# A decoder trunk on one core: the expert stage's candidate sums, selection steps, last U tiles, Gelu product and norm affine are issued in another way

## The chip, the cores and the metric

The kernel runs on one core of one Trainium2 chip. The metric is the device time of one execution in microseconds (us). A core has TensorE (matrix products, PE), VectorE (DVE), ScalarE (ACT), GpSimd (POOL) and the queues of SyncE (SP), which here issue the loads; each takes its own instructions in order.

## The reference

Two layers; x is 256 tokens by 1024 channels. In each layer two token mixers come first, then a feed-forward stage of 16,384 experts of one neuron each (PEER). The change touches the latter and the layer norm behind it:

```python
q = (h @ w_pq).reshape(B, S, PEER_HEADS, 2, half)             # 8 heads, two halves
s1, s2 = (einsum('bshd,hnd->bshn', q[..., i, :], sub_keys[i]) for i in (0, 1))   # 128 keys each
v1, i1 = lax.top_k(s1, 16);  v2, i2 = lax.top_k(s2, 16)
cand = v1[..., :, None] + v2[..., None, :]                    # 16 x 16 sums
top, pos = lax.top_k(cand, 16);  gates = softmax(top)
act = gelu(einsum('btd,bthkd->bthk', h, peer_u[idx]))         # idx: the 16 pairs' experts
y = einsum('bthk,bthkd->btd', gates * act, peer_v[idx])
x = layer_norm(ALPHA * x + y * gt2, ln_g, ln_b)
```

(The first lines are drawn together from several of the reference.)

## The kernel before

The kernel gathers nothing: it multiplies h by all of peer_u and takes gates that are zero but for the chosen experts. It holds fp32 accuracy by splitting every operand in two (h and lo, `wh` and `wl`) and adding three products. `peer` does this in four stages a layer.

- **U.** `u_tile(j)` for the 128 tiles of 128 experts: 24 products of 128x256 into a bank `A`, two tiles to a bank, two banks. `take` fetches, turns and splits tiles ahead. A tile is turned in one of two ways: a `u` tile by a stream transpose on VectorE (L220), an `x` tile by eight transposes on TensorE into bank `T` (L251), which ScalarE then copies twice over. In `uv_seq` every fourth tile is an `x`. Then ScalarE writes `wh` (L58) and GpSimd the rest, `wl` (L271).
- **Top-k, beside U.** `topk` is a generator: `pull`, behind each tile, lets it issue work of a given cost (1.55 a tile, 2.75 behind an x tile). For each of 16 units (a head, a block of 128 tokens) `key_ops` finds the 16 largest of two rows of 128 scores, and `cand_ops` of the unit before, interleaved with it, adds the two lists (L1400, 64 and 48 sums that can matter) and finds the 16 largest sums. The scores come through bank `K`, copied by ScalarE one unit ahead. Then the selection (L1444 to L1488) turns positions into expert numbers and gates, for each block of tokens, with operations on 128x2048 elements (L1465, L1468, L1470) twice.
- **Placement, beside U.** `place_gates`, in 64 blocks of four tokens: `build` compares (L1499) and multiplies (L1504) on VectorE, `prod` makes eight products into a bank `G`, `put` lays them into the expert-by-token buffer: a copy by ScalarE where the Gelu values are not there yet, a product by VectorE where they are (L1531). `fin_u` does the rest: it writes Gelu values of a finished pair of tiles, and where gates already stand multiplies by them (L1618).
- **V.** For the 128 tiles of peer_v VectorE and ScalarE split the gated values (`o`) and the weights, TensorE adds into four `Y` banks. In this stage GpSimd loads the norm's gain and bias (L434) and applies them to x, as two operations of 128x1024 for each half of the tokens (L1727, L1728).

The schedule is the order in which the Python issues instructions; no planner reorders it.

## Time and profile before

| | us |
|---|---|
| median of 3 runs (2248.74 to 2251.46) | 2249.8 |
| profiled execution | 2254.38 |
| its span | 2252.6 |
| TensorE busy | 2135.2 (95%) |
| VectorE busy | 1817.2 (81%) |
| ScalarE busy | 1172.5 (52%) |
| GpSimd busy | 1041.5 (46%) |

Busy shares are means over stages with different limits, so the stages are read one by one. In layer 0 U starts at about 303 us and V at 777; in layer 1 at about 1407 and 1883. A matmul's record overlaps the next one, so the pace of the products is read from their starts.

### The profile page before, as it was taken

Reading aid. Unit: us, or ns where it says so; the run is one execution under the profiler, and the core shown is the slowest. Engines: PE = TensorE matmul, PEld = TensorE weight load, DVE = VectorE, ACT = ScalarE, POOL = GpSimd, SP = SyncE. Lnnn points to the kernel's source line nnn. Section 1 sums busy time; section 2 is a strip of 40 time slices with the busy share of each in tenths; the row PEclk is TensorE's granted clock in tenths of the full one; section 3 lists DMA queues with packets and bytes.
Section 4 is the critical chain, followed back from the end, with each engine's and each line's share of the span. In section 5 each row is a group of like instructions: output and inputs, shape, how many; then the busy total and the mean of one; then the engine's idle time right before and its main releaser. Section 6 shows DMA issues by size and latency. Waiting matters only on the chain.

```text
span 2252.6 us, 42211 instructions
## 1 busy us (share of the span) xinstructions
PE 2135.2 (95%) x14596; PEld 1945.4 (86%) x14596; DVE 1817.2 (81%) x3278; ACT 1172.5 (52%) x2445; POOL 1041.5 (46%) x760
## 2 busy tenths in 40 slices
PE   5789899899999999999989998998999999999998
PEld 5789799899999978888779897997999999788886
DVE  7887989999997488888887558999999955666675
ACT  3446555455555545555545564554555555455562
POOL 4656637787778510000045534577777783200001
PEclk8999999999999999999999999999999999999999
DMA  8646567666667678888844335675766676666662
GB/s 273 196 137 221 159 140 159 129 148 148 142 147 156 176 236 275 281 286 283 298 134 150 113 121 142 147 153 118 154 142 148 146 164 187 202 196 192 193 227 90
DMA packets 498895, 400.32 MB, mean 178 GB/s; under 512 B 291920, under 2 KB 446072, under 8 KB 498680
## 3 DMA queue, kind: packets, MB, share of 16 engines
q1 hardware_dynamic: 496936, 392.33, 62.8%
q0 software_dynamic: 1408, 4.23, 0.6%
q8 instruction: 115, 1.88, 0.3%
q10 hardware_dynamic: 336, 1.06, 0.1%
q14 instruction: 100, 0.82, 0.1%
HBM read 396.46 MB, written 1.05 MB: 176 GB/s over the span
## 4 chain that ended last, share of the span: by engine, by line
PE 73%; DVE 16%; DMA 4%; issue 3%; ACT 3%; POOL 1%; SPq 1%; POOLq 0%; ACTq 0%; DVEq 0%
PE A L61 28%; PE Y L61 27%; PE T L61 7%; PE G L61 4%; PE T L251 2%; DVE wl L271 2%; PE ss L61 2%; PE hs L61 2%; DMA raw<-in_peer_u_dram 2%; POOL wl L271 1%; DVE qk L857 1%; DMA raw<-in_peer_v_dram 1%; DVE raw L220 1%; DVE e L843 1%; DVE o L1504 1%
## 5 line engine op out<-in xcount | busy, mean ns | idle before, releaser
L271 POOL TENSOR_TENSOR wl<-raw,wh 128x512 fp32r<-128x512 f32 x663 | 914.3, 1406 | 700.9 <-ACT wh L58 582.4
L58 ACT ACTIVATE wh<-raw 128x512 fp32r<-128x512 f32 x1060 | 610.8, 623 | 182.0 <-PE A L61 47.6
L61 PE MATMUL A<-hTh,wh 128*128 128x256 f32 x2080 | 543.3, 293 | 11.9 <-ACT wh L58 11.8
L61 PE MATMUL A<-hTl,wh 128*128 128x256 f32 x2080 | 524.2, 284 | 0.0
L61 PE MATMUL Y<-wh,o 128*128 128x512 f32 x1776 | 480.5, 392 | 0.8 <-DVE o L521 0.8
L271 DVE TENSOR_TENSOR wl<-raw,wh 128x512 fp32r<-128x512 f32 x525 | 380.2, 765 | 63.5 <-ACT wh L58 44.9
L61 PEld LDWEIGHTS A<-hTh,wh 128*128 128x128 f32 x2080 | 400.6, 193 | 14.4 <-ACT wh L58 13.7
L61 PEld LDWEIGHTS A<-hTl,wh 128*128 128x128 f32 x2080 | 401.7, 193 | 0.8 <-DVE hTl L521 0.2
L61 PEld LDWEIGHTS Y<-wh,o 128*128 128x128 f32 x1776 | 334.9, 189 | 70.8 <-DVE o L521 1.2
L61 PE MATMUL A<-hTh,wl 128*128 128x256 f32 x2080 | 337.9, 285 | 11.0 <-POOL wl L271 10.9
L61 PEld LDWEIGHTS A<-hTh,wl 128*128 128x128 f32 x2080 | 288.9, 193 | 14.2 <-POOL wl L271 14.2
L61 PE MATMUL Y<-wl,o 128*128 128x512 f32 x888 | 277.9, 393 | 10.4 <-DVE wl L271 10.4
L220 DVE STREAM_TRANSPOSE raw<-raw 128x1024 f32<-128x1024 f32 x192 | 235.1, 1230 | 11.7 <-DMA raw<-in_peer_u_dram 10.1
L58 ACT ACTIVATE o<-buf 128x256 fp32r<-128x256 f32 x228 | 95.1, 417 | 282.7 <-PE Y L61 282.7
L521 DVE TENSOR_TENSOR o<-buf,o 128x256 fp32r<-128x256 f32 x228 | 100.1, 439 | 150.4 <-ACT o L58 150.4
L61 PEld LDWEIGHTS Y<-wl,o 128*128 128x128 f32 x888 | 168.1, 189 | 48.9 <-DVE wl L271 13.8
L1499 DVE TENSOR_TENSOR o<-iT,iota_t 128x1024 f16<-128x1024 f16 x128 | 163.9, 1280 | 0.0
L58 ACT ACTIVATE buf<-G 128x128 f32<-128x128 f32 (+4 forms) x244 | 56.0, 276 | 203.6 <-PE G L61 203.6
L570 POOL TENSOR_TENSOR x<-x,buf 128x1024 f32<-128x1024 f32 x1 | 2.4, 2392 | 291.0 <-DVE x L567 291.0
L61 PE MATMUL T<-hTh,wh 128*128 128x256 f32 x512 | 133.6, 293 | 0.0
L61 PE MATMUL T<-hTl,wh 128*128 128x256 f32 x512 | 130.1, 286 | 0.0
L1504 DVE TENSOR_TENSOR o<-gT,o 128x1024 f16<-128x1024 f16 x128 | 124.6, 973 | 4.4
(496 smaller groups left out, 3254.9 us busy)
## 6 DMA issues: line engine op xcount, KB each, us to landing
raw<-in_peer_u_dram SPq DMA_DIRECT2D x1024, 128.0 KB, 3.5
raw<-in_peer_v_dram SPq DMA_DIRECT2D x256, 512.0 KB, 4.4
raw<-in_w_in_dram SPq DMA_DIRECT2D x88, 512.0 KB, 4.9
raw<-in_w_ada_dram SPq DMA_DIRECT2D x78, 512.0 KB, 4.9
raw<-in_w_o_dram SPq DMA_DIRECT2D x16, 512.0 KB, 3.5
raw<-in_w_pq_dram SPq DMA_DIRECT2D x64, 128.0 KB, 3.4
qk<-in_w_ada_dram SPq DMA_DIRECT2D x10, 512.0 KB, 3.9
e<-in_w_ada_dram SPq DMA_DIRECT2D x8, 512.0 KB, 6.0
```

Of the source, the lines that this page charges most:

```text
L58: nc.scalar.activation(o, i, f, **kw)
L61: nc.tensor.matmul(o, a, b, start=start, stop=stop, **kw)
L220: nc.vector.transpose(t, t)
L251: nc.tensor.transpose(banks[s][:, q], t[:, (4 * s + q) * P:(4 * s + q + 1) * P], ident)
L271: eng.tensor_sub(lo, src, h.bitcast(F32))
L521: nc.vector.tensor_sub(lo, src, h.bitcast(F32))
L570: nc.gpsimd.tensor_mul(xt[tt], xt[tt], last[0])
L843: eng.tensor_sub(ev[:, :, :hn], mid, bv[:, :, :hn])
L857: nc.vector.tensor_mul(tv[:, :, hn:], nodes(qT, n)[:, :, hn:], ev[:, :, hn:])
L1499: nc.vector.tensor_tensor(o.rearrange("p a u n v -> p (a u) n v"), iT[:, b].rearrange("p a (u v) -> p (a u) v", v=2)[:, :, None] .to_broad ...
L1504: nc.vector.tensor_mul(og.rearrange("p u a n v -> p (u a) n v"), gT[:, b * nu:(b + 1) * nu].rearrange("p u a v -> p (u a) v")[:, :, None] ...
```

## The change

Five edits, all in or beside `peer`:

1. `cand_ops` has ScalarE copy the first list of 16 values into a PSUM tile `vp` (a bank of `G`, taken when the search begins), and the additions read it there instead of in SBUF.
2. The selection yields after single operations, with higher costs, so that fewer of them are issued behind one tile.
3. `x` tiles end at tile 100: tiles 103, 107, ... 127 become `u` tiles, seven a layer.
4. `fin_u` of a finished pair is issued behind the `pull` of the even tile instead of ahead of it.
5. GpSimd's two times two operations on x become sixteen of 128x256, written behind V tiles 38 to 53.

```diff
-    uv_seq = [("x" if j % 4 == 3 else "u", j) for j in range(NK)] + [("v", j) for j in range(NK)]
+    uv_seq = [("x" if j % 4 == 3 and j < 100 else "u", j) for j in range(NK)] + [("v", j) for j in range(NK)]
...
+                    vp = psk.tile([P, 2, PH, TOPK], F32, name="G")
...
+                        act(vp[:, tt, h], v[0][tt][:, h], AF.Copy)
+                        yield 0.0
                         for a0, a1, w in segs:
...
-                                                 v[0][tt][:, h, a0:a1, None].to_broadcast(dims),
+                                                 vp[:, tt, h, a0:a1, None].to_broadcast(dims),
...
                             nc.vector.tensor_scalar(sel[a].bitcast(U32), puf, 4 - 2 * a, None,
                                                     op0=OP.logical_shift_right)
+                            yield 0.5
                             nc.vector.tensor_copy(half[2 + a], iu[a][tt].rearrange("p h k -> p (h k)").bitcast(U32))
+                            yield 0.6
...
-                        yield 0.9
+                        yield 0.5
...
-                            yield 1.4
+                            yield 1.7
                             nc.vector.tensor_mul(m, m, per_head(half[2 + a])[:, :, None].to_broadcast(k4))
                             yield 1.1
                             nc.vector.tensor_reduce(per_head(sel[a]), m, axis=mybir.AxisListType.X, op=OP.add)
-                            yield 1.4
+                            yield 1.6
...
-                    if pend:
-                        fin_u(*pend.pop())
                     if j % 2 == 1:
                         pend.append((j - 1, ps))
...
                     u_tile(j)
+                    old = [pend.pop(0)] if len(pend) > j % 2 else []
                     pull(sides, 1.55 + 1.2 * (kind == "x"))
+                    for f in old:
+                        fin_u(*f)
...
-                    if j in (NB_J + 6, NB_J + 12):
-                        xb = from_blocks(xt[j // 6 - (NB_J + 6) // 6])
-                        nc.gpsimd.tensor_mul(xb, xb, in_blocks(g_row))
-                        nc.gpsimd.tensor_add(xb, xb, in_blocks(b_row))
+                    n = j - NB_J - 6
+                    if 0 <= n < 16:
+                        xb = from_blocks(xt[n // 8])[:, n % 4]
+                        (nc.gpsimd.tensor_add if n // 4 % 2 else nc.gpsimd.tensor_mul)(
+                            xb, xb, in_blocks(b_row if n // 4 % 2 else g_row)[:, n % 4])
```

The first place is VectorE in the search of layer 0, around one unit's additions (`buf_3125` is the buffer with scores, lists and sums, `G` the bank with the copied list). Before:

```order
L1384 MAX buf_3125<-buf_3125 128x8
L1400 TENSOR_TENSOR buf_3125<-buf_3125 128x64
L1384 MAX buf_3125<-buf_3125 128x8
L1400 TENSOR_TENSOR buf_3125<-buf_3125 128x48
L1387 MAX_INDEX buf_3125<-buf_3125 128x8
```

Both additions read SBUF alone here. In the changed kernel, on the same engine at the same place:

```order
L1386 MAX buf_3125<-buf_3125 128x8 x2
L1404 TENSOR_TENSOR buf_3125<-G,buf_3125 128x64
L1389 MAX_INDEX buf_3125<-buf_3125 128x8
L1404 TENSOR_TENSOR buf_3125<-G,buf_3125 128x48
L1389 MAX_INDEX buf_3125<-buf_3125 128x8
```

The additions keep their places but for one operation, and read `G`. The copy that they wait for stands on ScalarE, in the same stretch, behind the score copy (`buf_3125<-K`) and sometimes behind the next tile's `wh`:

```order
L58 ACTIVATE buf_3125<-K 128x256
L58 ACTIVATE buf_3123<-A 128x512
L58 ACTIVATE wh<-raw 128x4x4x32 x2
L58 ACTIVATE G<-buf_3125 128x16
L58 ACTIVATE wh<-raw 128x4x4x32 x2
L58 ACTIVATE buf_3125<-K 128x256
L58 ACTIVATE G<-buf_3125 128x16
```

The row `G<-buf_3125` is new; the Gelu values (`buf_3123<-A`) now stand behind the score copy.

The second place is VectorE in the selection of layer 0, its first half, with the stream transposes of the U tiles between. Before:

```order
L1453 TENSOR_SCALAR buf_3125<-buf_3125 128x128
L1455 CAST buf_3125<-buf_3125 128x128
L1453 TENSOR_SCALAR buf_3125<-buf_3125 128x128
L1455 CAST buf_3125<-buf_3125 128x128
L1457 SCALAR_TENSOR_TENSOR buf_3125<-buf_3125 128x128
L1460 SCALAR_TENSOR_TENSOR buf_3125<-buf_3125 128x128 x2
L1461 SCALAR_TENSOR_TENSOR buf_3125<-buf_3125 128x128
L220 STREAM_TRANSPOSE raw<-raw 128x1024
L1465 TENSOR_TENSOR buf_3125<-buf_3125,iota_k 128x2048
L1468 TENSOR_TENSOR buf_3125<-buf_3125 128x2048
L1470 TENSOR_REDUCE buf_3125<-buf_3125 128x128
L220 STREAM_TRANSPOSE raw<-raw 128x1024
```

No transpose stands within the small operations, and none within the three large ones. In the changed kernel, on the same engine from the same operation on:

```order
L1457 TENSOR_SCALAR buf_3125<-buf_3125 128x128
L1460 CAST buf_3125<-buf_3125 128x128
L220 STREAM_TRANSPOSE raw<-raw 128x1024
L1457 TENSOR_SCALAR buf_3125<-buf_3125 128x128
L1460 CAST buf_3125<-buf_3125 128x128
L1463 SCALAR_TENSOR_TENSOR buf_3125<-buf_3125 128x128
L1467 SCALAR_TENSOR_TENSOR buf_3125<-buf_3125 128x128 x2
L220 STREAM_TRANSPOSE raw<-raw 128x1024
L1469 SCALAR_TENSOR_TENSOR buf_3125<-buf_3125 128x128
L1473 TENSOR_TENSOR buf_3125<-buf_3125,iota_k 128x2048
L1476 TENSOR_TENSOR buf_3125<-buf_3125 128x2048
L220 STREAM_TRANSPOSE raw<-raw 128x1024
```

One transpose now stands within the small operations, one behind them, and one within the large ones. From the end of the search to the first block's comparison there were 11 transposes and 15 tiles, now there are 14 and 19; the last block's products come behind tile 105 before, behind tile 110 now.

The third place is VectorE in the placement, from the transpose of an even tile on. Before:

```order
L220 STREAM_TRANSPOSE raw<-raw 128x1024
L1618 TENSOR_TENSOR buf_3124<-A,buf_3124 128x2x76
L1499 TENSOR_TENSOR o_6590<-iT,iota_t 128x1024
L1504 TENSOR_TENSOR o_6592<-gT,o_6590 128x1024
L1531 TENSOR_TENSOR buf_3123<-G,buf_3123 128x32x4
L1531 TENSOR_TENSOR buf_3124<-G,buf_3124 128x30x4
```

The product (L1618) stands ahead of the block's comparison (L1499). In the changed kernel, some blocks on, on the same engine:

```order
L220 STREAM_TRANSPOSE raw<-raw 128x1024
L1507 TENSOR_TENSOR o_6771<-iT,iota_t 128x1024
L1512 TENSOR_TENSOR o_6773<-gT,o_6771 128x1024
L1539 TENSOR_TENSOR buf_3123<-G,buf_3123 128x32x4
L1539 TENSOR_TENSOR buf_3124<-G,buf_3124 128x30x4
L1626 TENSOR_TENSOR buf_3124<-A,buf_3124 128x2x80
```

The product that reads the bank `A` moved from the front of the block to its end. On GpSimd the sixteen pieces follow one another with no other instruction between them, behind the two loads of gain and bias, and wait for those loads only.

## Rows read from the trace of the kernel before

**Rows 1.** Windows of 100 us: the stretch, its length, then each engine's busy time with its instructions, TensorE's granted clock as a share of full speed, the share of the DMA engines and GB/s. In order: the search's end and the selection of layer 0, its placement, the end of its U stage, and the search's end and the selection of layer 1.

```profile
400.00:500.00 100.00, 90.67 (x739) 87.86 (x739) 97.08 (x158) 48.70 (x100) 77.27 (x53) 0.97 0.65 138
...
600.00:700.00 100.00, 99.83 (x929) 97.66 (x928) 97.98 (x147) 54.95 (x146) 77.71 (x56) 1.00 0.64 144
700.00:800.00 100.00, 99.97 (x759) 95.69 (x759) 51.70 (x73) 54.19 (x105) 61.14 (x48) 1.00 0.70 175
...
1500.00:1600.00 100.00, 88.50 (x713) 85.23 (x711) 97.86 (x171) 47.76 (x96) 74.23 (x52) 0.97 0.64 132
```

**Rows 2.** Windows of 20 us in the selection, of layer 0 and of layer 1, with the same columns.

```profile
420.00:440.00 20.00, 15.55 (x98) 14.52 (x97) 19.83 (x14) 8.80 (x15) 14.64 (x9) 0.83 0.36 80
...
1520.00:1540.00 20.00, 12.51 (x80) 11.06 (x79) 19.72 (x22) 8.42 (x16) 12.18 (x7) 0.91 0.35 88
...
1560.00:1580.00 20.00, 18.55 (x141) 18.05 (x140) 19.80 (x19) 9.37 (x17) 17.18 (x12) 0.91 0.52 114
```

**Rows 3.** Windows early in the V stage, of layer 0 and of layer 1, with the same columns.

```profile
826.00:836.00 10.00, 7.91 (x29) 6.08 (x28) 9.73 (x10) 4.36 (x9) 4.08 (x3) 0.85 0.83 269
836.00:846.00 10.00, 6.46 (x21) 4.65 (x20) 9.75 (x7) 1.46 (x3) 6.39 (x3) 0.84 0.43 145
...
1935.00:1950.00 15.00, 10.26 (x37) 7.50 (x36) 12.40 (x10) 4.34 (x9) 10.01 (x6) 0.86 0.50 144
```

**Rows 4.** Timeline of ScalarE and of VectorE in layer 0 (start, duration, engine, line, operation, output and inputs, shapes, count; in brackets the idle time before it and what ended it): three score copies, then the first maximum of the search, two candidate additions, the first operation of the selection and the first comparison of the placement.

```profile
320.05 0.38 ACT L58 ACTIVATE buf<-K 128x256 f32<-128x256 f32 x1 [3.56 <-PE K L61]
...
329.97 0.38 ACT L58 ACTIVATE buf<-K 128x256 f32<-128x256 f32 x1 [3.10 <-PE K L61]
...
400.71 0.38 ACT L58 ACTIVATE buf<-K 128x256 f32<-128x256 f32 x1 [1.12 <-PE K L61]
...
321.47 0.44 DVE L1384 MAX8 buf<-buf 128x8 f32<-128x128 f32 x2
...
327.66 0.23 DVE L1400 TENSOR_TENSOR buf<-buf 128x64 f32<-128x64 f32 x1
...
398.94 0.69 DVE L1400 TENSOR_TENSOR buf<-buf 128x64 f32<-128x64 f32 x1
...
416.27 0.13 DVE L1444 COPY buf<-buf 128x8 f32<-128x8 f32 x1
...
470.62 0.64 DVE L1499 TENSOR_TENSOR o<-iT,iota_t 128x1024 f16<-128x1024 f16 x1
```

**Rows 5.** VectorE in the search of layer 0: groups by form between 320 and 420 us (busy us, mean ns), then all 32 candidate additions (minimum, median and maximum of their durations in ns), then the timeline: one addition on VectorE, the pair of subtractions on GpSimd at that time, and a product of Gelu values and gates later on.

```profile
L220 DVE STREAM_TRANSPOSE raw<-raw 128x1024 f32<-128x1024 f32 x20 | 24.5, 1225 | 0.0
...
L1400 DVE TENSOR_TENSOR buf<-buf 128x48 f32<-128x48 f32 x16 | 12.3, 768 | 0.0
...
L1400 DVE TENSOR_TENSOR buf<-buf 128x64 f32<-128x64 f32 x16 | 7.7, 481 | 0.0
...
L1400 DVE TENSOR_TENSOR buf<-buf x32: 178/380/1306, 324.0 to 412.1; 128x64 f32<-128x64 f32 x16, 128x48 f32<-128x48 f32 x16
...
339.36 1.27 DVE L1400 TENSOR_TENSOR buf<-buf 128x64 f32<-128x64 f32 x1
...
338.01 2.54 POOL L271 TENSOR_TENSOR wl<-raw,wh 128x512 fp32r<-128x512 f32 x2 [0.42 <-ACT wh L58]
...
478.16 0.17 DVE L1618 TENSOR_TENSOR buf<-A,buf 128x8 f32<-128x8 f32 x1 [0.34 <-ACT A L58]
```

**Rows 6.** The chain of work that ended last, in the last U tiles of layer 0, where no placement runs (start, duration, engine, tile and line, matmuls): 96 products are four tiles, and the x tile's transposes lie between two rows.

```profile
709.29 11.51 PE A L61 x96
721.68 11.51 PE A L61 x96
```

**Rows 7.** Timeline in the selection of layer 0: TensorE at the first tile that it waits for, two operations on 2048 elements on VectorE, and GpSimd's subtractions.

```profile
418.19 0.39 PE L61 MATMUL A<-hTh,wh 128*128 128x256 f32 x1 [2.24 <-ACT wh L58]
...
422.02 2.24 DVE L1465 TENSOR_TENSOR buf<-buf,iota_k 128x2048 f16<-128x2048 f16 x1
...
450.55 1.18 DVE L1468 TENSOR_TENSOR buf<-buf 128x2048 f16<-128x2048 f16 x1
...
430.81 14.71 POOL L271 TENSOR_TENSOR wl<-raw,wh 128x512 fp32r<-128x512 f32 x10 [3.19 <-ACT wh L58]
```

**Rows 8.** Timeline in the placement of layer 0: on TensorE the products of three blocks (four tiles lie between the first and the second), on VectorE a product of Gelu values and gates and the second half of the build behind it.

```profile
602.51 0.63 PE L61 MATMUL G<-o,o 128*128 128x128 f16 x8
...
617.13 0.63 PE L61 MATMUL G<-o,o 128*128 128x128 f16 x8
...
620.72 0.63 PE L61 MATMUL G<-o,o 128*128 128x128 f16 x8
...
617.54 0.44 DVE L1618 TENSOR_TENSOR buf<-A,buf 128x312 f32<-128x312 f32 x1
...
619.00 1.67 DVE L1504 TENSOR_TENSOR o<-gT,o 128x1024 f16<-128x1024 f16 x1
```

**Rows 9.** Timeline early in the V stage of layer 0: GpSimd's first operation on x, and three pairs of subtractions on VectorE.

```profile
828.91 2.37 POOL L1727 TENSOR_TENSOR x<-x,buf 128x1024 f32<-128x1024 f32 x1
...
827.98 3.85 DVE L271 TENSOR_TENSOR wl<-raw,wh 128x512 fp32r<-128x512 f32 x2
...
832.09 1.28 DVE L271 TENSOR_TENSOR wl<-raw,wh 128x512 fp32r<-128x512 f32 x2
...
837.40 5.62 DVE L271 TENSOR_TENSOR wl<-raw,wh 128x512 fp32r<-128x512 f32 x2
```

More of the change, by code (lines that the diff above doesn't have):

```diff
@@ L1454, in topk @@
                                                     op0=OP.logical_shift_right)
+                            yield 0.5
                             nc.vector.tensor_copy(half[2 + a], iu[a][tt].rearrange("p h k -> p (h k)").bitcast(U32))
+                            yield 0.6
                         nc.vector.scalar_tensor_tensor(half[0], sel[1].bitcast(U32), -12.0, sel[0].bitcast(U32),
                                                        op0=OP.add, op1=OP.max)
+                        yield 0.5
                         for a in range(2):
                             nc.vector.scalar_tensor_tensor(sel[a], half[0], -16.0 + 12 * a, puf, op0=OP.mult, op1=OP.add)
+                            yield 0.5
                         nc.vector.scalar_tensor_tensor(half[1], sel[1], -48.0, sel[0], op0=OP.add, op1=OP.max)
                         tp = top[tt]
-                        yield 0.9
+                        yield 0.5
                         for a in range(2):
```

## The prediction, made before the changed kernel had run

> **What bounds the kernel now.** I read the windows first, then the chain of work that ended last, then the timelines of the stretches that stood out. TensorE is the bound: in the middle of either expert stage it is busy 99.83 of 100 us [rows 1]. Time can be won where it idles, and where it does work that another engine has room for. In layer 0 it idles 9.33 us between 400 and 500, in layer 1 11.50 us between 1500 and 1600 [rows 1]; there VectorE is busy 97 to 98 of 100. The granted clock also falls, to 0.83 and 0.91 of full speed [rows 2]: 15.55 us of busy time at 0.83 would have been 12.9 at full clock, so 2.6 us are lost in layer 0, and 1.1 + 1.7 = 2.8 us by the two windows of layer 1. These two stalls cost 11.9 + 14.3 = **26.2 us**. The other idle place is early in the V stage: 2.09 + 3.54 us in layer 0 and 4.74 us in layer 1, with clocks of 0.84 to 0.86 that cost 1.2 + 1.0 and 1.4 us by the same working [rows 3], **14.0 us** together. The first is the end of the top-16 search and the selection behind it; the second is GpSimd's four operations on x.
>
> **Why the first stall is there.** A unit of the search (one head, one block of tokens) lets VectorE work from 321.47 to 416.27 us for 16 units, 5.93 us each; TensorE's pace is that of the score copies, 15 steps from 320.05 to 400.71, 5.38 us each [rows 4]. VectorE falls behind 0.55 us a unit. Part of it is the candidates' addition: 768 and 481 ns on average where the shortest of the 32 took 178 [rows 5]. The long ones end when GpSimd's subtraction ends: the one that starts at 339.36 and lasts 1.27 us ends at 340.63, GpSimd's pair started at 338.01 and lasted 2.54, to 340.55 [rows 5]. Both read two operands from SBUF. Then the selection puts 54.4 us of VectorE work (416.27 to 470.62, with 11 stream transposes) beside 15 U tiles, for which TensorE needs 15 x 2.88 + 3 x 0.87 = 45.8 us (2.88 is a quarter of 11.51, and 0.87 the rest of the step of 12.39 us for four tiles, which is the x tile's eight transposes) [rows 4, 6]. VectorE is 8.6 us too long there, and GpSimd with it: ten subtractions took 14.71 us at 430.81, 1.47 each instead of 1.27 [rows 5, 7].
>
> **1. The copy to PSUM.** The additions then have one operand in PSUM. The nearest row is the product of Gelu values and gates, PSUM and SBUF in: 0.17 us for eight elements while GpSimd works in that stretch too [rows 5]. I take 0.2 us for either addition, so a unit loses 1.25 - 0.40 = 0.85 us and comes to 5.08, below TensorE's 5.38. A price against it: DVE's overhead is about 60 ns on SBUF and 125 ns on PSUM by the Trainium skill (Perfetto Trace Analysis, Optimizing Scalar/DVE Operations), which would be an estimate of 32 x 0.065 = 2 us a layer and a result 4 us higher; the row of 0.17 us, not longer than the shortest two-SBUF addition, speaks against it.
> The 16 copies a layer are small work for ScalarE, which is half idle (busy 55 of 100 us even in the placement [rows 1]): nothing by themselves. But they add a wait. The copy stands behind the next unit's score copy, which waits for TensorE to end the current tile; the addition, and behind it on VectorE the rest of the unit and the next stream transpose (hence ScalarE's wh, GpSimd's wl, TensorE), now waits for that. In the trace the addition of the second candidate unit ran at 327.66, and the score copy that it will stand behind ended at 329.97 + 0.38 [rows 4]: VectorE will be held there by some 3 us. So the gain doesn't pile up over 16 units; VectorE follows TensorE's pace about 0.6 us behind each score copy. The last such copy ends at 401.09. The addition that will stand behind it ran at 398.94 and the search ended 17.3 us later, at 416.27 [rows 4]; three units without port waits save 2.6 us of that. From 401.09 + 0.6 on, the search ends at 416.4, as now: **0** by itself, and no stall of TensorE in the search, since a unit stays 0.3 us under its pace. Bounds: the end could come 3 us earlier, if the last units hold more port waits than the mean, and 3 us later, if each of the 16 waits adds 0.2 us that I don't see.
>
> **2. The finer steps of the selection.** By the order the first product of the placement now comes 19 tiles after the search instead of 15, with 14 stream transposes instead of 11. VectorE: 54.4 + 3 x 1.2 = 58.0 us. TensorE: 19 x 2.88 + 4 x 0.87 = 58.2. The 8.6 us excess goes. What is left are lumps: two operations on 2048 elements still stand between two transposes, 2.24 us each where GpSimd holds its operands, 1.18 where not [rows 7]. Three places decide. Tile 28 waits 2.24 us for its transpose now [rows 7], and still will if the search ends no earlier. From there to the transpose of tile 34 VectorE has five transposes (6 us), small operations of 3 to 5 us, two lumps of 2.4 to 4.5 us and a reduction of 2.24: 16 to 22 us against TensorE's 6 x 2.88 + 0.87 = 18.2; to that of tile 42 it has 10.6 to 14.8 us against 12.4. So between 0 and 2.2 + 4 + 2.4 = 8.6 us are left in a layer; I take 4, clock included, since with half the excess gone GpSimd and VectorE hold each other less. The stalls go from 26.2 to 8, **-18 us**; bounds -9 and -26.
>
> **3. Seven x tiles a layer become u tiles.** Each takes 0.87 us of transposes off TensorE and adds one stream transpose (1.225 us) to VectorE [rows 5, 6]; ScalarE loses two copies, SP issues four DMAs either way. Where no placement runs VectorE has room: in 700 to 800 it is busy 51.7 of 100 [rows 1]. By the order that holds for tiles 115, 119, 123 and 127: 4 x 0.87 = 3.5 us a layer. But the placement, begun four tiles later, now ends behind tile 110 instead of 105, so tiles 103 and 107 and the transpose of 111 fall into it. There four tiles with their blocks and one x take TensorE 14.62 us (602.51 to 617.13) [rows 8], 13.75 without the x, and VectorE is busy 97.98 of 100 [rows 1]. With a transpose for every tile VectorE needs 14.62 + 1.2 = 15.8 us for four tiles, 2.1 more than TensorE. Over the eleven blocks behind tiles 98 to 110 that is up to 6 us, less some 3 us spared in the two tiles that carry no block: the 3 x 0.87 us are eaten. I take 3 us a layer, **-6 us**; bounds 0 and -12.
>
> **4. The product behind the placement.** VectorE's sum is the same. The product no longer stands ahead of the block's comparison: in the trace the build that starts behind it, with its second half of 1.67 us at 619.00, ends at 620.67, just as TensorE starts on it at 620.72 [rows 8], so this gets 0.4 us more room. But the bank of A comes back later: the product that ran at 617.54 would now end 0.44 us behind the placement, near 621.5, and TensorE wants the bank behind the block (0.63 us from 620.72) and an x tile's transposes (0.87), near 622.2 [rows 6, 8]. So some 0.7 us are left. I count **0**; its price if that cover goes is a rival.
>
> **5. GpSimd's x in sixteen pieces.** The code spreads them over sixteen V tiles, but by the order GpSimd has nothing between them and no wait on the V loop: they run back to back as soon as the rows have landed, as the four do now. An operation of 1024 elements takes 2.37, of 512 1.27 us [rows 5, 9], so a piece of 256 some 0.7, 11.5 us in all instead of 9.5. Now VectorE is held for a whole operation at a time: pairs of subtractions took 3.85 and 5.62 us instead of 1.28 [rows 9]. With pieces each hold is 0.7 us, but there are four times as many, one for each operation of VectorE. VectorE's lead is under 1 us there (the first pair lost 2.57 us, and TensorE idled 2.09 [rows 3, 9]), so what is lost in small pieces is lost to TensorE all the same, but for what VectorE's idle time between tiles makes up. I take **0**; bounds +5 and -6.
>
> **The sum.** -18 - 6 = -24 us against the profiled execution, whose span is 2252.6 us (2254.4 with what lies around it). The runs' median is 2249.8, so I forecast **2226 us**.
>
> **Rivals.** (a) The pieces free the V stage. If a wait of 0.7 us is covered by VectorE's lead each time, TensorE doesn't stall and its clock holds: 12 of the 14.0 us come back, 2214. For it: each hold is short. Against it: the lead of less than 1 us. The Trainium skill (Perfetto Trace Analysis, Optimizing Scalar/DVE Operations) says that breaking up instructions may let work be completed sooner where an unsaturated engine causes bubbles; by that it would come out so. Chance 0.15.
> (b) The new wait keeps the old stall. VectorE, held to the score copies, enters the selection no earlier, the lumps cost the full 8.6 us and more a layer, and the x tiles return nothing: -2 to -10, 2240 to 2248, half of it within 0.2% of now. For it: the lead of 3 us that it gives up. Chance 0.18.
> (c) Slower: the bank of A. If the product ends over 0.7 us beyond where I put it (another hold by GpSimd, 1.3 us, would do), TensorE waits at the first matmul of every pair of tiles in the placement, 32 pairs a layer. At 0.6 us each with both layers that is +38 us against -24: 2264. For it: VectorE has no slack in that stage. Against it: the sums above. Chance 0.05.
> The edits that may not do what they say are 3, in part, and 5; both stand in the forecast that way.
>
> **How the numbers follow.** Forecast 0.62, with 2214 to 2238 by the bounds of parts 2, 3 and 5 taken together; (a) 0.15, (b) 0.18, (c) 0.05. A measurement of this kernel can tell about 0.2% (4.5 us) from no change. Faster: 0.62 + 0.15 + half of (b) = 0.86; same 0.09; slower 0.05. The range 2209 to 2242 takes in (a) and the better part of (b), and leaves out (c), the rest of (b) and a little below.
>
> **What would show it.** In the search: additions of 0.2 us, and waits of VectorE for ScalarE of 2 to 3 us. At 400 to 500 and 1500 to 1600: TensorE idle 2 to 4 us instead of 9.3 and 11.5. In the last tiles of U: four tiles in 11.5 us. At the placement's end: VectorE full and TensorE with short waits for its blocks. In the V stage: sixteen pieces in a row, and idle time of TensorE as before. It is wrong if TensorE waits for the bank of A, or if the idle time after the search stays above 6 us a layer.

## The result and the profile after

The changed kernel took 2234.7 us (median of 4 runs, 2233.52 to 2234.87) where the kernel before took 2250.12 beside it (4 runs): a ratio of 0.9929, with a 95% interval of 0.9913 to 0.9944. The profiled execution went from 2254.38 to 2234.87, its span from 2252.6 to 2233.1. The gain is 15.4 us by the medians, where 24 were forecast.

First the windows of the kernel after, with the columns of [rows 1]: the search's end and the selection of layer 0, its placement, the end of its U stage, and the selection of layer 1; then three of 20 us in the selection (two of layer 0, one of layer 1) and two of 10 us early in V, which answer to [rows 2, 3].

```profile
400.00:500.00 100.00, 93.77 (x775) 91.51 (x773) 94.27 (x149) 52.20 (x104) 84.87 (x57) 0.98 0.69 148
...
600.00:700.00 100.00, 95.96 (x893) 93.54 (x891) 99.07 (x147) 52.51 (x138) 80.33 (x54) 1.00 0.62 144
700.00:800.00 100.00, 98.60 (x739) 93.61 (x740) 69.34 (x97) 51.85 (x101) 61.76 (x46) 1.00 0.61 176
...
1500.00:1600.00 100.00, 93.75 (x780) 91.46 (x779) 95.90 (x145) 52.34 (x105) 85.03 (x57) 0.98 0.68 147
...
420.00:440.00 20.00, 18.68 (x138) 17.91 (x137) 19.86 (x13) 8.15 (x15) 19.94 (x12) 0.91 0.52 124
460.00:480.00 20.00, 18.45 (x153) 18.04 (x152) 19.65 (x18) 9.42 (x17) 19.78 (x14) 1.00 0.76 161
1500.00:1520.00 20.00, 17.96 (x137) 17.55 (x136) 19.66 (x68) 12.70 (x23) 14.62 (x11) 0.91 0.66 152
...
826.00:836.00 10.00, 8.19 (x29) 6.25 (x28) 8.56 (x9) 3.73 (x9) 7.54 (x9) 0.83 0.84 279
836.00:846.00 10.00, 8.75 (x37) 6.24 (x36) 10.00 (x11) 4.05 (x10) 8.07 (x8) 1.00 0.61 191
```

Three things are to be seen. TensorE's idle time around the selection fell from 9.33 and 11.50 us [rows 1] to 6.23 and 6.25, not to the 2 to 4 expected, and in layer 0 GpSimd is now busy 19.94 and 19.78 of 20 us there. The placement, where TensorE idled 0.17 us of 100 [rows 1], now idles 4.04 (600 to 700). GpSimd's work in the selection is a train without a break (GpSimd's timeline in the selection of layer 0):

```profile
418.31 23.80 POOL L271 TENSOR_TENSOR wl<-raw,wh 128x512 fp32r<-128x512 f32 x14 [3.72 <-ACT wh L58]
```

And early in V the idle time of the two windows is 3.06 us instead of 5.63 [rows 3], with the granted clock at 1.00 in the second, where it was 0.84.

What TensorE waited for in the U stage of layer 0 (waits view from 290 to 780 us: total, times, longest), and what VectorE's additions waited for in both layers:

```profile
PE G L61 <- DVE o L1512: 4.9, 13, 0.9
PE A L61 <- POOL wl L271: 4.3, 8, 1.0
PE A L61 <- DVE buf L1626: 3.1, 3, 1.8
PE A L61 <- ACT wh L58: 1.9, 1, 1.9
...
DVE buf L1404 <- ACT G L58: 20.9, 14, 2.4
```

The same view of the kernel before, from 290 to 780 us:

```profile
PE A L61 <- POOL wl L271: 5.4, 7, 1.3
PE A L61 <- ACT wh L58: 3.7, 2, 2.2
```

(A row of 0.3 us, the same in both, is left out of either.) The waits for the build (`o`) and for the bank that the Gelu product reads (L1626) are new. The waits for `wl` and `wh` are the old stall, 9.1 us before and 6.2 after. More than half of it in layer 0 was a wait for GpSimd (`wl`) already before the change; what the change shortened most is the wait for `wh`, which hangs on VectorE's transposes. The additions wait for ScalarE as predicted, up to 2.4 us.

Where a stage begins and ends can be read to 0.01 us in every trace: U from the first transposition into `A`, V from the first product into `Y`. These lengths are used in what follows (us; the kernels are those of the experiments below; "between" is V of layer 0 and the next mixers, "last" V of layer 1 to the end):

| profile | U, layer 0 | between | U, layer 1 | last |
|---|---|---|---|---|
| before | 476.7 | 626.7 | 479.5 | 369.6 |
| after | 473.4 | 622.7 | 472.6 | 363.8 |
| no4 | 469.9 | 624.2 | 469.1 | 363.7 |
| gelu_early | 471.2 | 623.9 | 471.2 | 363.8 |
| no1 | 478.3 | 622.4 | 479.0 | 363.8 |
| only1 | 478.2 | 627.9 | 476.4 | 368.5 |
| only2 | 473.6 | 626.2 | 474.2 | 369.3 |
| no24 | 471.4 | 626.1 | 469.3 | 363.8 |
| no3 | 475.5 | 624.2 | 474.9 | 363.8 |
| cut112 | 468.3 | 627.4 | 467.5 | 363.7 |
| no5 | 473.4 | 626.6 | 473.0 | 369.4 |
| psum_sel | 467.1 | 623.3 | 466.3 | 363.7 |
| best | 465.7 | 624.8 | 464.8 | 362.8 |

From before to after the U stages lost 3.3 and 6.9 us, V and what lies behind it 4.0 and 5.8.

Each length is that of one execution. "Between" holds the same code in eight of these kernels (all with part 5 but best), and reads 622.4 to 627.4 there, while "last" reads 363.7 to 363.8 in the same eight. So a single length can differ by some us without a change in its own code, and a difference of 1 to 3 us is an indication, a better one where both layers and the waits agree. The profile of the kernel before lies 4.3 us above its median, so the four losses add up to 19.5 us where the medians give 15.4.

### The profile page after: what moved, and what is told of

It is laid out like the page before. It is cut to its first block, busy times and chain, and to the rows that moved or that the text cites. A ratio compares the mean times of both kernels' runs of the same rounds, so it can differ in the third digit from the quotient of the medians.

```text
span 2233.1 us, 42093 instructions
## 1 busy us (share of the span) xinstructions
PE 2117.2 (95%) x14484; PEld 1928.4 (86%) x14484; DVE 1825.5 (82%) x3294; ACT 1167.0 (52%) x2443; POOL 1081.9 (48%) x784
## 4 chain that ended last, share of the span: by engine, by line
PE 66%; DVE 18%; DMA 6%; issue 3%; ACT 3%; POOL 2%; SPq 1%; POOLq 0%; DVEq 0%; ACTq 0%
PE Y L61 28%; PE A L61 22%; PE T L61 7%; DMA raw<-in_peer_u_dram 4%; PE G L61 3%; PE ss L61 2%; DVE wl L271 2%; POOL wl L271 2%; PE hs L61 2%; DVE o L1512 2%; PE T L251 2%; DVE raw L220 2%; DVE o L1507 2%; DVE qk L857 1%; DVE e L843 1%
## 5 line engine op out<-in xcount | busy, mean ns | idle before, releaser
L271 POOL TENSOR_TENSOR wl<-raw,wh 128x512 fp32r<-128x512 f32 x663 | 944.0, 1448 | 654.1 <-ACT wh L58 609.0
L58 ACT ACTIVATE wh<-raw 128x512 fp32r<-128x512 f32 x1088 | 627.6, 622 | 187.6 <-PE A L61 59.0
L220 DVE STREAM_TRANSPOSE raw<-raw 128x1024 f32<-128x1024 f32 x206 | 252.7, 1232 | 4.4 <-DMA raw<-in_peer_u_dram 3.8
L58 ACT ACTIVATE buf<-G 128x128 f32<-128x128 f32 (+26 forms) x238 | 54.4, 274 | 206.4 <-PE G L61 206.4
L1512 DVE TENSOR_TENSOR o<-gT,o 128x1024 f16<-128x1024 f16 x128 | 155.5, 1215 | 4.4
L1507 DVE TENSOR_TENSOR o<-iT,iota_t 128x1024 f16<-128x1024 f16 x128 | 145.4, 1136 | 0.0
```

The costliest lines, as they stand in the source:

```text
L58: nc.scalar.activation(o, i, f, **kw)
L220: nc.vector.transpose(t, t)
L271: eng.tensor_sub(lo, src, h.bitcast(F32))
L1507: nc.vector.tensor_tensor(o.rearrange("p a u n v -> p (a u) n v"), iT[:, b].rearrange("p a (u v) -> p (a u) v", v=2)[:, :, None] .to_broad ...
L1512: nc.vector.tensor_mul(og.rearrange("p u a n v -> p (u a) n v"), gT[:, b * nu:(b + 1) * nu].rearrange("p u a v -> p (u a) v")[:, :, None] ...
```

## The experiments

All are compared with the kernel before run beside them; its median moved between 2250.1 and 2253.1 us from one group of runs to another, so the ratios are compared, 0.0001 being 0.23 us. Each ratio has an interval of some 0.0015 either way (only1: 0.0009), so that two kernels' difference is known to about 0.002, 5 us; below that the stage lengths and the waits can only hint.

**The late product (part 4): no4 and gelu_early.** no4 undoes part 4:

```diff
-                    old = [pend.pop(0)] if len(pend) > j % 2 else []
                     pull(sides, 1.55 + 1.2 * (kind == "x"))
-                    for f in old:
-                        fin_u(*f)
```

and `if pend: fin_u(*pend.pop())` stands again within `u_tile`.

> The changed kernel (2234.7 us) with the product of Gelu values and gates put back ahead of the block's work. Theory: the late product is what the placement pays for. In the changed kernel TensorE waits there for the build (o) 4.9 us in layer 0 and 3.7 in layer 1, and for the bank of A 3.1 and 2.1 us; four tiles take 14.85 us instead of 14.62. With the product ahead again both kinds of wait go, four tiles take 14.62 us again, and the time is 2234.7 - 13.8 = 2221 us if all of it goes, 2227 if the waits at the placement's end, which may be the last u tiles' doing, stay. Rival: the waits come from the placement's later start against the tiles (the finer selection), so they stay, and the time is 2233 to 2236 us.

gelu_early splits `fin_u`: the Gelu values and `progress["j"]` come ahead of the `pull`, VectorE's product behind it.

```diff
                     if T0 > 0:
                         act(ps[:, :, :T0], ps[:, :, :T0], AF.Gelu)
+                    progress["j"] = j + 2
+                    yield
+                    if T0 > 0:
                         nc.vector.tensor_mul(sl[:, :, :T0], ps[:, :, :T0], sl[:, :, :T0])
-                    progress["j"] = j + 2
...
-                    old = [pend.pop(0)] if len(pend) > j % 2 else []
+                    old = [fin_u(*pend.pop(0))] if len(pend) > j % 2 else []
+                    for f in old:
+                        next(f)
                     pull(sides, 1.55 + 1.2 * (kind == "x"))
                     for f in old:
-                        fin_u(*f)
+                        list(f)
```

> The changed kernel with ScalarE's Gelu values issued ahead of the block's work again and VectorE's product left behind it: ScalarE's order is then that of no4, VectorE's differs from it by the product's place alone. The kernel before took 2252 us in the runs beside no4, no4 2229, and the changed kernel by its ratio of 0.9929 would be 2236. Theory: what costs the 7 us is ScalarE's order, which delays wh, so that GpSimd's subtractions fall on two of VectorE's builds in four tiles instead of one; here they don't, and the time is no4's, 0.9894 of before, 2229 us. Rival: VectorE's order does it (the bank of A comes back behind the placement, and the tiles' transposes later): 0.993, 2236 us.

Measured: no4 0.9894 (0.9879 to 0.9909), 7.9 us better than the changed kernel; gelu_early 0.9889 (0.9874 to 0.9904), the same as no4. So the product's place on VectorE costs nothing that can be told. What costs is what gelu_early puts back: the Gelu values' place on ScalarE, and with it that of `progress["j"]`, by which `put` chooses between ScalarE and VectorE for a tile; the two were not moved apart. The waits agree: for the banks `A` and `G` TensorE waits 14.2 and 12.1 us in the two U stages of the changed kernel, 10.7 and 10.8 in gelu_early, 10.4 and 10.0 in no4. ScalarE around the Gelu values of a pair in the placement (timeline), after:

```profile
598.90 0.39 ACT L58 ACTIVATE buf<-A 128x256 f32<-128x256 f32 x1
599.32 0.37 ACT L58 ACTIVATE A<-A 128x256 f32<-128x256 f32 x1
599.60 1.14 ACT L58 ACTIVATE wh<-raw 128x512 fp32r<-128x512 f32 x2
```

and before, where `wh` came first:

```profile
600.08 1.15 ACT L58 ACTIVATE wh<-raw 128x512 fp32r<-128x512 f32 x2
601.12 0.36 ACT L58 ACTIVATE buf<-A 128x232 f32<-128x232 f32 x1
601.52 0.39 ACT L58 ACTIVATE A<-A 128x280 f32<-128x280 f32 x1
```

The groups of VectorE and of GpSimd from 520 to 680 us (busy us, mean ns), after:

```profile
L1512 DVE TENSOR_TENSOR o<-gT,o 128x1024 f16<-128x1024 f16 x43 | 51.2, 1191 | 1.5
L1507 DVE TENSOR_TENSOR o<-iT,iota_t 128x1024 f16<-128x1024 f16 x43 | 47.6, 1107 | 0.0
...
L271 POOL TENSOR_TENSOR wl<-raw,wh 128x512 fp32r<-128x512 f32 x88 | 131.0, 1511 | 32.5 <-ACT wh L58 30.7 <-ACT raw L58 0.6
```

and in gelu_early:

```profile
L1507 DVE TENSOR_TENSOR o<-iT,iota_t 128x1024 f16<-128x1024 f16 x43 | 54.5, 1268 | 0.0
L1512 DVE TENSOR_TENSOR o<-gT,o 128x1024 f16<-128x1024 f16 x44 | 42.3, 962 | 1.5
...
L271 POOL TENSOR_TENSOR wl<-raw,wh 128x512 fp32r<-128x512 f32 x88 | 124.6, 1437 | 36.2 <-ACT wh L58 21.6 <-ACT raw L58 14.7
```

A block's two operations take 1191 + 1107 = 2298 ns after and 2230 in gelu_early, and a subtraction 1511 against 1437: the two engines hold each other longer. With Gelu's two operations ahead of `wh` on ScalarE, GpSimd starts its subtractions later and runs four in a row (timeline of GpSimd, after):

```profile
600.30 6.26 POOL L271 TENSOR_TENSOR wl<-raw,wh 128x512 fp32r<-128x512 f32 x4 [1.28 <-ACT wh L58]
607.92 5.95 POOL L271 TENSOR_TENSOR wl<-raw,wh 128x512 fp32r<-128x512 f32 x4 [1.35 <-ACT wh L58]
```

Here the second half of two of four builds takes 1.66 us (those at 602.50 and 611.06), where one of four did before. One thing stays with VectorE's order: at the placement's end gelu_early still waits 3.1 us for the bank of `A`; but no4 waits 3.0 us there for the build, so this is one excess of VectorE in two forms.

**The copy to PSUM (part 1): no1 and only1.** no1 takes part 1 out of the changed kernel, only1 puts it alone into the kernel before; the edit is that of the change.

> The changed kernel (2234.7 us) with the candidate additions on SBUF alone. The prediction counted this edit at 0 (bounds 3 us each way): 2235 us. Rival: the search ends 2.7 us later again in layer 0 and 3.5 us in layer 1, measured from the start of U, and TensorE, which idles behind it, ends later by as much: +6 us, 2241 us.

> The kernel before with the candidate lists copied to PSUM, and nothing else. The prediction: 0, 2252 us. Theory from no1 and no2: this edit carries most of what the search and the selection gained (0.0042 of the time, 9.4 us): 2243 us, with a search that ends 3 us earlier in either layer and VectorE idle for ScalarE in it.

Measured: no1 0.9971 (0.9960 to 0.9983), 9.5 us worse than the changed kernel, more than the rival's 6; only1 0.9982 (0.9973 to 0.9991), a gain of 4 us, between the two expectations. Its search ends 113.5 us behind the start of U in either layer. All candidate additions of layer 0 (minimum, median, maximum in ns), after and then no1:

```profile
L1404 DVE TENSOR_TENSOR buf<-G,buf x32: 169/209/226, 324.8 to 411.0; 128x64 f32<-128x64 f32 x16, 128x48 f32<-128x48 f32 x16
```

```profile
L1400 DVE TENSOR_TENSOR buf<-buf x32: 178/884/1316, 324.4 to 416.1; 128x64 f32<-128x64 f32 x16, 128x48 f32<-128x48 f32 x16
...
424.04 0.39 PE L61 MATMUL A<-hTh,wh 128*128 128x256 f32 x1 [4.11 <-ACT wh L58]
```

With PSUM they are short whatever GpSimd does. Without it their median is 380 ns before [rows 5] and 884 in no1, where the late Gelu values have moved the subtractions onto them (in the search no1 differs from the kernel before in part 4 alone): the search ends 119.7 us behind the start of U (420.24 - 300.50), before it was 116.2 (416.27 - 300.11), after 113.5 (414.10 - 300.60), and TensorE waits 4.11 us at once. So part 1 is worth 4 us alone and 9.5 beside the other parts: there it also covers the harm that part 4 does in the search.

**The finer steps (part 2): only2, no2 and no24.** only2 is the kernel before with part 2 alone, no2 the changed kernel without it, no24 the kernel no4 without it.

> The kernel before with the finer steps of the selection, and nothing else. The prediction: 18 us less, 2234 us (bounds 9 and 26 less). Theory from no2: the stall behind the search loses 2 to 3 us a layer, and the placement, four tiles later, gives nothing back since it isn't VectorE's stage alone: 5 us less, 2247 us. A second rival: nothing at all, 2252.

> The changed kernel (2234.7 us) with the old, coarser steps of the selection. Theory (the prediction's): VectorE's excess of 8.6 us a layer over TensorE comes back, less the 2.7 and 3.5 us by which the search now ends earlier: idle time of TensorE and lost clock around the selection rise from 6 to 7 us a layer to 12 or more, +10 us, 2245 us (the placement also starts four tiles earlier, which the x tiles' end at 100 then leaves with less VectorE work at its end: up to 4 us less). Rival: what shortened the stall is the earlier end of the search, and not the steps: 2234 to 2237 us.

> The kernel no4 (2229 us, 0.9894 of before) with the old, coarser steps of the selection as well: edits 1, 3 and 5 alone. Theory from the profiles (only2 against before: U stage 3.1 and 5.3 us shorter): the finer steps are worth 3 to 5 us a layer wherever the late product doesn't eat them: 2236 us. Rival from the medians (no2 as fast as the changed kernel): once the search has given its 3 us back they are worth nothing, 2229 us.

Measured: only2 0.9956 (0.9942 to 0.9969), 9.9 us, at the weak bound of the prediction and twice what the theory from no2 gave; no2 0.9926 (0.9913 to 0.9940), as fast as the changed kernel; no24 0.9896 (0.9879 to 0.9913), as fast as no4: the rival's number in both. The single runs of no2 lie between 2233.9 and 2241.1 us, and its profile is of the slowest, so its lengths aren't used; no24's U stages are 1.5 and 0.3 us longer than no4's. The waits of TensorE in the U stage of layer 0 show where the gain went (400 to 500 us, then 680 to 730). In no24:

```profile
PE A L61 <- POOL wl L271: 5.4, 7, 1.3
PE A L61 <- ACT wh L58: 4.6, 3, 1.9
...
PE G L61 <- DVE o L1508: 1.0, 1, 1.0
```

and in no4, between 680 and 730:

```profile
PE G L61 <- DVE o L1512: 3.0, 3, 1.3
```

Between 400 and 500 no4 waits 6.8 us (its rows stand with psum_sel), no24 10.0. The finer steps save 3.2 us in the selection, start the placement four tiles later, and lose 2.0 at its end, among the tiles that part 3 gave to VectorE; in layer 1 they save 1.7 and lose 2.0. In only2 those are `x` tiles still, and its U stages keep 3.1 and 5.3 us. That part 3 is what takes the gain is read from these waits; no run has parts 1 and 2 without part 3, and part 1's earlier search, the rival's reason, may have its share.

**The last u tiles (part 3): no3 and cut112.** no3 takes part 3 out of the changed kernel; cut112 is no4 with `j < 112` for `j < 100`.

> The changed kernel (2234.7 us) with x tiles to the end of U again. Theory: the four tiles of a layer that lie behind the placement give back 4 x 0.87 us, and the three within it cost more in waits of TensorE at the placement's end (for the bank of A 3.1 and 2.1 us, for the build 1.1 and 0.3 us, in the two layers) than the 2 x 2.6 us that they spare: 2 x 3.5 + 5.2 - 6.6 = +5.6, so 2240 us, without waits for the bank of A. Rival: the waits at the placement's end have nothing to do with the kind of the tiles and stay; then all seven tiles return, 14 x 0.87 = +12, 2247 us.

> The kernel no4 (2229 us, 0.9894 of before) in which x tiles end at 112 instead of 100: tiles 103, 107 and 111 are x tiles again. The prediction: what these three spare TensorE, 2.6 us a layer, VectorE loses at the placement's end, so no difference, 2229 us; the waits of TensorE for the build, 3.0 us a layer at 680 to 730 in no4, go, and its transposes come in their place. Rival: they did spare something, +5 us, 2234; second rival: VectorE's excess there cost more than they spared, 2225.

Measured: no3 0.9943 (0.9929 to 0.9956), 3.2 us worse than the changed kernel, within what can be told; by the stage lengths 2.0 and 2.4 us. Both are nearer to the theory's 5.6 than to 12, and the wait for the bank of `A` is 0.2 us, as the theory had it. cut112 0.9881 (0.9864 to 0.9897), 2.9 us better than no4, within what can be told; but its U stages are 1.6 us shorter in both layers, and between 680 and 730 us TensorE waits for nothing. ("Between" is 3.2 us longer in its profile, so that the whole spans differ by 0.3 us only.) By these lengths tiles 103, 107 and 111 as `u` tiles cost 1.6 us a layer, and the four behind the placement save about 3.6 to 4.0 (2.0 or 2.4, and 1.6).

**The pieces (part 5): no5.** The changed kernel with the four whole operations on x.

> The changed kernel (0.9929 of before) with GpSimd's four whole operations on x in place of sixteen pieces. Theory: the pieces are what shortened the idle time early in V (5.63 + 4.74 us before, 3.06 + 1.57 after, and the clock fell less); it comes back: +6 us, 0.9955. Rival, the prediction's: the pieces follow one another just the same, and the idle time depends on where VectorE stands when they begin: no difference, 0.993.

Measured: 0.9956 (0.9942 to 0.9970), 6.1 us worse: the theory. The two profiles differ by 9.5 us behind the U stages, 5.6 of them in "last", the length that scatters least: it is 363.7 to 363.8 us in eight kernels with the pieces and 368.5 to 369.6 in the four without. VectorE and GpSimd early in V, layer 0, after (timeline):

```profile
824.51 4.28 DVE L271 TENSOR_TENSOR wl<-raw,wh 128x512 fp32r<-128x512 f32 x2
...
836.28 2.37 DVE L271 TENSOR_TENSOR wl<-raw,wh 128x512 fp32r<-128x512 f32 x2
...
825.45 2.79 POOL L1738 TENSOR_TENSOR x<-x,buf 128x256 f32<-128x256 f32 x4
830.71 13.36 POOL L1738 TENSOR_TENSOR x<-x,buf 128x256 f32<-128x256 f32 x12 [2.46 <-DMA buf<-in_ln_b_dram]
```

and no5:

```profile
833.34 5.62 DVE L271 TENSOR_TENSOR wl<-raw,wh 128x512 fp32r<-128x512 f32 x2
...
839.01 0.70 PE L61 MATMUL Y<-wl,o 128*128 128x512 f32 x1 [2.25 <-DVE wl L271]
```

Twelve pieces stretch over 13.36 us, and a pair of VectorE's subtractions costs 2.37 us among them instead of 5.62. The first four hold a pair for 4.28 us, nearly as a whole operation did.

**What is left of the stall: psum_sel.** no4 with the broadcast operands of the selection's large operations in PSUM.

```diff
-                    vp = psk.tile([P, 2, PH, TOPK], F32, name="G")
+                    vp = psk.tile([P, 3, PH, TOPK], F32, name="G")
+                    act(vp[:, 2, 0], iota_k, AF.Copy)
...
-                            nc.vector.tensor_copy(half[2 + a], iu[a][tt].rearrange("p h k -> p (h k)").bitcast(U32))
+                            nc.vector.tensor_copy(vp[:, a].rearrange("p h k -> p (h k)"), iu[a][tt].rearrange("p h k -> p (h k)").bitcast(U32))
...
-                                                    iota_k[:, None, None].to_broadcast(k4), op=OP.is_equal)
+                                                    vp[:, 2, 0][:, None, None].to_broadcast(k4), op=OP.is_equal)
...
-                            nc.vector.tensor_mul(m, m, per_head(half[2 + a])[:, :, None].to_broadcast(k4))
+                            nc.vector.tensor_mul(m, m, vp[:, a][:, :, None].to_broadcast(k4))
```

> The kernel no4 (2229 us, 0.9894 of before) in which the two operations on 2048 elements of the selection take their broadcast operand (the numbers 0 to 15, and the list of key numbers) from PSUM, in the bank that holds the candidate lists. Theory: what is left of the stall behind the search is GpSimd's: in 423 to 441 us of no4 it runs ten subtractions without a break in 17.86 us, 1.79 each instead of 1.27, because it takes turns with VectorE's operations on two SBUF operands; two of them are more than a tile of 2.88 us, and TensorE waits for wl 6.6 us a layer. With PSUM operands the subtractions take 1.3 us there, the operations on 2048 elements about the 2.2 us that they take now, and the waits go: 10 us less, 2219 us. Rival: VectorE's own sum is the limit (the prediction's reading), and since its operations aren't shorter nothing changes: 2228 us. Second rival: an operation that reads PSUM is longer, 2.6 us or more, and the time rises by 4 x 0.4 x 2 = 3 us a layer or more: 2235.

Measured: 0.9861 (0.9845 to 0.9878), 2222.1 us, 7.4 us better than no4. GpSimd in the selection, and TensorE's waits from 400 to 500 us, in no4:

```profile
423.37 17.86 POOL L271 TENSOR_TENSOR wl<-raw,wh 128x512 fp32r<-128x512 f32 x10 [2.37 <-ACT wh L58]
...
PE A L61 <- POOL wl L271: 6.6, 9, 1.5
PE A L61 <- ACT wh L58: 0.2, 1, 0.2
```

and in psum_sel, with two operations of VectorE:

```profile
438.74 10.16 POOL L271 TENSOR_TENSOR wl<-raw,wh 128x512 fp32r<-128x512 f32 x8 [3.11 <-ACT wh L58]
...
PE A L61 <- ACT wh L58: 2.4, 2, 1.2
PE A L61 <- POOL wl L271: 0.8, 5, 0.2
...
432.15 2.25 DVE L1474 TENSOR_TENSOR buf<-buf,G 128x2048 f16<-128x2048 f16 x1
434.44 2.29 DVE L1477 TENSOR_TENSOR buf<-buf,G 128x2048 f16<-128x2048 f16 x1
```

A subtraction takes 1.27 us instead of 1.79, VectorE's operations the 2.2 to 2.3 us that they took (with the operand in PSUM the multiplication takes that everywhere; where nothing held it, it took 1.18 [rows 7]), and the wait for `wl` falls from 6.6 to 0.8 us. 2.4 us for `wh`, which is VectorE's part, remain. That is the theory, with 7.4 of its 10 us (5.5 by the U stages).

**The best together: best.** psum_sel with cut112's tiles, and the addition of each quarter behind its multiplication.

```diff
-                        xb = from_blocks(xt[n // 8])[:, n % 4]
-                        (nc.gpsimd.tensor_add if n // 4 % 2 else nc.gpsimd.tensor_mul)(
-                            xb, xb, in_blocks(b_row if n // 4 % 2 else g_row)[:, n % 4])
+                        xb = from_blocks(xt[n // 8])[:, n // 2 % 4]
+                        (nc.gpsimd.tensor_add if n % 2 else nc.gpsimd.tensor_mul)(
+                            xb, xb, in_blocks(b_row if n % 2 else g_row)[:, n // 2 % 4])
```

> The kernel psum_sel (0.9861 of before, 2222 us) with x tiles to 112 as in cut112 and with the sixteen pieces in another order: the addition of each quarter right behind its multiplication, instead of four multiplications and then four additions. Theory: cut112 shortened each U stage by 1.6 us by the traces (the wait for the build of 3.0 us went, transposes came), so -3.2; and the first four pieces, which find the gain there while the second row is still on its way, hold VectorE's pair of subtractions for 4.1 to 4.3 us, for which TensorE waits 1.3 us in layer 1 and 1.8 to 2.4 in layer 0: a single piece, followed by a wait for the second row, would hold it for 2 us, and these waits go, another -3. Together 2216 us, 0.9834. Rival: the pair is held by whatever stands in GpSimd's queue at that moment, and later pieces take the place of the first four: 2219 us, 0.9847.

Measured: 0.9867 (0.9850 to 0.9883), 2219.8 us: by the ratio no better than psum_sel, by the stage lengths 1.4 + 1.5 us in U and 0.9 in the last stage. GpSimd in V, layer 1:

```profile
1905.15 0.75 POOL L1738 TENSOR_TENSOR x<-x,buf 128x256 f32<-128x256 f32 x1
1909.57 15.73 POOL L1738 TENSOR_TENSOR x<-x,buf 128x256 f32<-128x256 f32 x15 [3.67 <-DMA buf<-in_ln_b_dram]
```

A single piece now runs ahead of the second row, and TensorE's wait for `wl` there went from 1.3 to 0.2 us. In layer 0 it still waits 2.3 us in five places (2.6 in three in psum_sel), and "between" is 1.5 us longer: the forecast's 6 us more did not come as a whole.

## Why the prediction was right, and where it wasn't

The direction and the range held. The mechanism did not as a whole: both things that the prediction names as signs of being wrong came to pass, as TensorE waited for the bank of `A`, and the idle time after the search stayed above 6 us a layer (6.23 and 6.25). The sum reads 0 for parts 1, 4 and 5 and -24 for 2 and 3. The runs give about -17 to -18 for parts 1 to 3 together (17.2 by the U stages of no4 against before, 17.8 by the ratio of no4 less part 5), +7.9 for part 4 and -6.1 for part 5, together -15.4 to -16.0, where the medians fell by 15.4. Two terms that were set to zero, of opposite sign, nearly cancel, and that is luck; some 7 of the 8.6 us missed are in parts 1 to 3.

- **The stall's bound.** It was read as VectorE's, 8.6 us too long, with GpSimd as a companion whose delay would ease. The step that failed is "with half the excess gone GpSimd and VectorE hold each other less". They held each other more: ten subtractions took 1.47 us each before [rows 7], and after the change 14 take 23.80 us, 1.70 each, 3.4 a tile of 2.88. GpSimd had become the bound, and psum_sel shows that it was the turns with VectorE that made it so. The trace before had it already: 5.4 of 9.1 us of waiting in layer 0 were for `wl`, and 1.47 us each is 2.94 a tile, above TensorE's 2.88. The Trainium skill (SBUF — State Buffer, Who interferes with whom) says that an operation of VectorE with two inputs in SBUF holds up one of GpSimd that reads SBUF, and the other way round, for a whole instruction, and that one with a single SBUF input, outside the two-port modes, doesn't. The trace agrees: GpSimd's subtractions take 1.79 us beside operations with two, 1.27 beside those with one.
- **Part 1, counted 0 with bounds of 3.** The search did end 2.7 and 3.5 us earlier (layer 1: 116.96 to 113.49 us behind the start of U), at the bound. The additions came to 0.2 us as said (209 ns in the median, 178 the shortest from SBUF), and not with the surcharge for PSUM of some 65 ns that the prediction takes from the Trainium skill (Perfetto Trace Analysis, Optimizing Scalar/DVE Operations). What the step lacked is that the cost of the old additions isn't a constant: it depends on where the subtractions fall, and part 4 moves these.
- **Part 2, counted -18.** Mis-sized: -9.9 alone, nothing that can be told beside the others. By the prediction's own working, idle time and lost clock, the stalls were to fall from 26.2 us to 8; they fell to 15.8 (6.23 + 1.7 and 6.25 + 1.6, the clock at 0.91 in one window of each layer). VectorE's 58.0 us for the selection came to 63.8 (414.10 to 477.94), and what remained of the gain was lost again at the placement's end.
- **Part 3, counted -6.** -3.2, as far as can be told. By the stage lengths the four tiles behind the placement gave about the 3.5 us a layer; the three within it did not come out even ("eaten") but cost 1.6 more.
- **Part 4, counted 0.** The step followed VectorE's queue, and that was right there (gelu_early). It did not follow ScalarE's, on which the moved step has two operations of 0.4 us, which now stand ahead of `wh`. Rival (c) looked for the bank of `A`; TensorE did wait for it, 3.1 and 2.1 us in the two layers, at the placement's end alone.
- **Part 5, counted 0.** The step that failed is "what is lost in small pieces is lost to TensorE all the same". Rival (a) was right in its mechanism and half right in its size, 6 us of 12. A pair that takes 1.1 us longer is mostly covered (TensorE waits 0.45, 0.17 and 0.64 us among the twelve). The Trainium skill (Perfetto Trace Analysis, Optimizing Scalar/DVE Operations) advises to break up instructions where ScalarE or VectorE, unsaturated, cause bubbles. It says so of those two engines; here it held for GpSimd's instructions, 6.1 us by no5.

## What to carry to other kernels

Where two engines hold each other for whole instructions, the cost of an operation is a matter of its place in time: moving anything that shifts one of the two queues, even on a third engine, re-deals it, and taking one operand out of the shared memory removes the lottery (additions of 166 to 240 ns in every kernel with the copy, up to 1366 without). When a step is moved, follow each queue on which it issues, the small one too. Gains that spend the same engine's room don't add: the finer steps were worth 9.9 us alone, and none that can be told beside edits that won time at the same stall and gave VectorE more work at the placement's end.

## What was not expected of the hardware

Four pieces of GpSimd in a row held one VectorE pair throughout (2.79 of 4.28 us), while the next twelve took turns with VectorE one for one (2.37 us a pair). Both times GpSimd's pieces stood ready in its queue; why the first four weren't interrupted stays open. best, where only one of them was ready, avoids it and doesn't explain it.
